# An up projection that goes over from raw to normalised input, two k-tiles a pair of products

## The chip, the cores and the metric

The kernel runs on one core of a Trainium2 chip. The metric is the device time of one execution in microseconds. The kernel before takes 1709.6 us (median of 3 runs, 1709.41 to 1709.67).

## What is computed

One layer of a decoder trunk for 288 tokens: 256 of a prompt and 32 of a sample group (8 sequences of 4). D_MODEL is 2048 and D_FF is 5632. All values are fp32. The part of the reference that the change is in:

```python
x1 = _layernorm(ALPHA * x + mixed @ w_out, ln1_g, ln1_b)
a, b = jnp.split(x1 @ w_up, 2, axis=-1)
a, conv_ffn_new = _causal_dwconv(a, conv_ffn_prev, w_conv_ffn)
y = _layernorm(ALPHA * x1 + (jax.nn.silu(a) * b) @ w_down, ln2_g, ln2_b)
```

What comes ahead of it (one large input projection, a gated short convolution, a dilated window attention, the output projection) is left as it is.

## The kernel before, in words

Features lie on the 128 partitions and tokens on the free axis, so a matrix of 2048 features by 288 tokens is 16 *k-tiles* of 128 x 288. TensorE multiplies in a reduced fp32 type, and each fp32 operand is therefore held as two parts, hi and lo. A *split* makes them: ScalarE (ACT) copies the value to hi, and VectorE (DVE) subtracts hi from the value, which is lo (`split`, one line for all its uses, L231). `mms` (L225 to L227) forms one block of 128 output features: for each of 16 k-tiles it issues three matmuls, hi by hi, hi by lo and lo by hi. Such a block is called a *product* here, of 48 matmuls, in one PSUM accumulator (`acc`, 6 buffers).

Weights stream from HBM, 1 MB a product. They are split in two halves of 8 k-tiles (`whi` by ACT, `wlo` by DVE, 4 buffers each), so that the weights of the next product are split while this one runs. Every engine executes its instructions in one fixed order. That order is not the order of the code: a scheduler makes it when the program is built, and it may put the matmuls of one product among those of its neighbours.

The FFN goes in three parts of 16, 16 and 12 *pairs*. Pair f has two products, a and b, each over the 16 k-tiles of x1: the first product gives a block of `a` (then convolution and Silu), the second a block of `b` (then `gated`: silu(a) times b, and a split of the result into `yah`, `yal`). After the pairs of a part come 16 *down products* that add their share to `dd`.

The layer norm between the mixer and the FFN needs all 16 k-tiles before its mean and variance are known. Part 0 does not wait for it: its 32 products multiply the raw `dd` times the gain g (held split in `xh`, `xl`), with two more columns per k-tile that hold g and b themselves. So a product of part 0 has 290 columns instead of 288 (`x_gb` against `x`). `normed` then applies the norm to the result: an ACT copy of the two extra columns (`wgb`), and two DVE operations (L1011 and L1012) that multiply by r and add the mean's term. Here r and nmr are the per-token factors that `n1.finish` makes.

Meanwhile `dd` itself is normalised in its place, one k-tile a pair: two additions or multiplications on GpSimd (POOL, L1051 and L1052), which `tc.issue_after` puts behind the copies L769 and L770 of that pair, and one on ACT (L1053). In part 0's down products the normalised `dd` is split back into `xh` and `xl`, one k-tile a down product. Parts 1 and 2 then multiply that in 288 columns, with no `normed`.

The steps of a pair, in the names of the trace: first product; ACT `wgb` L1009; DVE `h` L1011, L1012; ACT `u` L1031 (two operations) and `cy` L755; POOL L769, L770 (the last rows, out of `u`), then L1051, L1052 and, for a later pair, L748, L750 (a memset and a copy into `u`); DVE convolution L757 (two); ACT Silu L1037; second product; `wgb`, L1011, L1012 again; DVE `gated` L782, L785; ACT `yah` and DVE `yal`, both L231.

Of the kernel before, what the change touches and what calls it, by code (L numbers as in the profile page):

```python
# [13 lines left out]
AF = mybir.ActivationFunctionType  # L14
ALU = mybir.AluOpType
# [5 lines left out]
KD = D // P  # L21
# [60 lines left out]
TILE_K = 2.5  # L82
VALUES_AT = 64
TILE_V = 2.5
LEAD = 4


# [10 lines left out]
def layer_kernel(ctx: ExitStack, tc: tile.TileContext, ins, outs):  # L98
    nc = tc.nc
    pe, dve, act, pool, sp = nc.tensor, nc.vector, nc.scalar, nc.gpsimd, nc.sync  # L100
# [42 lines left out]
    def behind(i, after):  # L143

        tc.add_manual_dep(i.ins, after.ins.name, no_sync, reason="pace")
# [7 lines left out]
    w_split = []  # L153
# [40 lines left out]
    last_mm = [None]  # L194
# [3 lines left out]
    def prompt_step():  # L198
        if prompt[0]:
            prompt[1] -= 1  # L200
            if prompt[1] <= 0:
                prompt[1] = next(prompt[0], None)
                if prompt[1] is None:
                    prompt[0] = None

    def product(x):
# [8 lines left out]
        mms(o, w, x)  # L215
        prompt_step()
        return o.rearrange("p a h -> p h a")

    def mms(out, w, x):
        nk = sum(n for _, _, n in w)  # L220
        k = 0
        for hi, lo, n in w:
            for c in range(n):
                xh_k, xl_k = (t[:, k].rearrange("p h a -> p a h") for t in x)
                pe.matmul(out, hi[:, c, :], xh_k, start=k == 0, stop=False)  # L225
                pe.matmul(out, hi[:, c, :], xl_k, start=False, stop=False)  # L226
                last_mm[0] = pe.matmul(out, lo[:, c, :], xh_k, start=False, stop=k == nk - 1)  # L227
                k += 1

    def split(hi, lo, src):  # L230
        return act.copy(hi, src), dve.tensor_tensor(lo, src, f32(hi), ALU.subtract)  # L231
# [9 lines left out]
    o = sb(ps, [P, T], "acc")  # L241
# [10 lines left out]
    xs = sb(big, [P, KD, T], "yah")  # L252
# [79 lines left out]
    x = (xh[:, :, :, :H], xl[:, :, :, :H])  # L332
    x_gb = (xh[:, :, :, :HG], xl[:, :, :, :HG])
# [25 lines left out]
    pa = sb(big, [P, KD * T], "yal")  # L359
# [49 lines left out]
    def in_a_row(row):  # L409

        for before, i in zip(row, row[1:]):
            behind(i, before)
# [362 lines left out]
    def gated(out, y, o, add=None):  # L775

        yt = y[:, SEQ : SEQ + NB * (NT + 2)].rearrange("p (b r) -> p b r", b=NB)
        for a, b, c in zip(of_halves(h2(out)), of_tokens(y[:, :SEQ], yt[:, :, 2:]), of_halves(o)):
            if add is None:
                dve.tensor_tensor(a, b, c, ALU.mult)  # L780
            elif len(a.shape) == 3:
                dve.scalar_tensor_tensor(a, c, add, b, ALU.add, ALU.mult)  # L782
            else:
                for h in range(2):
                    dve.scalar_tensor_tensor(a[:, h], c[:, h], add, b[:, h], ALU.add, ALU.mult)  # L785

    cm = sb(big, [P, KD, 2 + 2 * NB], "cm")
    for i in range(KD):
        ph = product(x)
        h = sb(wk, [P, T], "h", bufs=2)  # L790
# [7 lines left out]
        y = conv(u, R_WCM + i * 3)  # L798
# [204 lines left out]
        n1.add(i)  # L1003
    n1.finish()

    def normed(o):
# [4 lines left out]
        dve.tensor_tensor(h2(t), o[:, :, :H], h2(n1.r), ALU.mult)  # L1011
        dve.scalar_tensor_tensor(t, n1.nmr, w[:, 0:1], t, ALU.mult, ALU.add)  # L1012
        return h2(t), w[:, 1:2]
# [3 lines left out]
    f = 0  # L1017
# [3 lines left out]
    for part, nf in enumerate(THIRDS):  # L1021
        gh = sb(big, [P, KD, T], "yah", F32R)
        gl = sb(big, [P, KD, T], "yal", F32R)
        for k in range(nf):
            pa = product(x_gb if part == 0 else x)
            u = sb(wk, [P, UW + 2], "u", bufs=2)
            up, us = conv_in(u[:, :UW], R_SF + f * 2 * NB)
            if part == 0:
                pa, b1 = normed(pa)
                for a, b in zip(of_tokens(up, us), of_halves(pa)):  # L1030
                    act.activation(a, b, AF.Identity, bias=b1)  # L1031
# [5 lines left out]
            act.activation(y, y, AF.Silu)  # L1037
            pb = product(x_gb if part == 0 else x)
            gf = sb(wk, [P, T], "ya", bufs=2)
            if part == 0:  # L1040
                gated(gf, y, *normed(pb))
            else:
                gated(gf, y, pb)
# [4 lines left out]
            if part == 0:  # L1048

                with tc.issue_after(i_rows.ins):  # L1050
                    pool.tensor_tensor(dd[:, k], dd[:, k], n1.r, ALU.mult)  # L1051
                    pool.tensor_tensor(dd[:, k], dd[:, k], n1.nmr, ALU.add)  # L1052
                act.activation(dd[:, k], dd[:, k], AF.Identity, bias=n1.at(n1.b, k), scale=n1.at(n1.g, k))  # L1053
        if f == KF:
            sp.dma_start(outs["o_cf"].rearrange("p (k r) -> p k r", k=KF), cf)
        for i in range(KD):
            o = product((h3(gh), h3(gl)))
            if part == 0:
                for i_x, *before in zip(split(x[0][:, i], x[1][:, i], h2(dd[:, i])), last_split, w_split):
                    for b in before:  # L1060
                        behind(i_x, b)
                dve.scalar_tensor_tensor(h2(dd[:, i]), h2(dd[:, i]), ALPHA, o, ALU.mult, ALU.add)
            else:
                if f == KF and i > 0:
                    i_c = pool.tensor_tensor(dd[:, i], dd[:, i], n2.c, ALU.subtract)
# [197 lines left out]
```

## Time and profile before

| | us |
|---|---|
| three timed runs, median | 1709.6 |
| the profiled execution | 1709.6 |
| its span | 1707.3 |
| TensorE busy in the span | 1700.1 |
| VectorE, ScalarE, GpSimd busy | 1166.9, 912.4, 281.9 |
| part 0, 32 up products (first matmul to last) | 914.93 to 1104.77 |

The profiled execution took what the timed runs took, and 2.3 us of it lie around the span. A profile's TensorE row says how long matmuls were in flight, not how fast they came: a matmul stands for 285 ns in the rows, but one starts every 123 ns, because they are pipelined. In rows of the timeline the columns are start (us from the span's start), duration (us; for a merged row from the first's start to the last's end), engine, line, operation, output<-inputs, shapes and count, and in brackets how long the engine had stood idle and what ended it. Wait rows are: who waited, for whom, us in total, times, longest. A group's row ends in busy us, mean ns of one, and idle time before.

### The profile page before, as it was taken

The page shows a single profiled execution, that of the slowest core. Times are in us where ns is not written, and L with a number is a line of the kernel's source. Part 1 is how long each engine was busy: PE and PEld are TensorE (multiplying, and loading weights), DVE is VectorE, ACT ScalarE, POOL GpSimd, SP SyncE. Part 2 cuts the span into 40 slices and gives each one's busy share as a digit, 9 for nine tenths or more (in the row PEclk, how much of TensorE's full clock was granted, in tenths as well). Part 3 has the DMA queues.
Part 4 walks back from the last instruction along what each step waited for, and adds up shares of the span by engine and source line. Part 5 has one row for each costly group of instructions (what it writes and reads, how often), then busy time and mean ns, then how long its engine had stood idle before and what let it go on. Part 6 is the DMA issues. An engine that isn't in the chain of part 4 may idle for free.

```text
span 1707.3 us, 34051 instructions
## 1 busy us (share of the span) xinstructions
PE 1700.1 (100%) x14110; PEld 1697.4 (99%) x14110; DVE 1166.9 (68%) x1619; ACT 912.4 (53%) x1546; POOL 281.9 (17%) x428
## 2 busy tenths in 40 slices
PE   9999999999999999999999999999999999999998
PEld 9999999999999999999999999999999999999998
DVE  6458998886877675455788888855556555555576
ACT  6356776565655554444546555644455543344455
POOL 0011111000000000011454332300110100011165
PEclk9999999999999999999999999999999999999999
DMA  8766776666767876778766767677677667766663
GB/s 299 281 249 238 255 262 250 233 248 229 258 242 254 312 274 247 266 289 332 272 254 250 261 247 250 249 269 269 249 256 260 248 248 256 274 257 249 246 225 112
DMA packets 61308, 436.19 MB, mean 255 GB/s; under 512 B 7841, under 2 KB 14241, under 8 KB 21537
## 3 DMA queue, kind: packets, MB, share of 16 engines
q1 hardware_dynamic: 59856, 430.19, 68.7%
q10 hardware_dynamic: 1296, 3.83, 0.7%
q8 instruction: 110, 1.80, 0.4%
q14 instruction: 46, 0.37, 0.1%
HBM read 427.53 MB, written 94.53 MB: 306 GB/s over the span
## 4 chain that ended last, share of the span: by engine, by line
PE 99%; DVE 0%; ACT 0%; ACTq 0%; DVEq 0%; issue 0%
PE acc L225 32%; PE acc L226 32%; PE acc L227 32%; PE acc L351 2%; DVE dd L972 0%; PE acc L243 0%; PE acc L621 0%; PE acc L421 0%; PE att L456 0%; PE acc L426 0%; PE att L467 0%; PE att L880 0%; PE att L882 0%; ACT yah L976 0%; ACT cache L941 0%; ACT cache L946 0%
## 5 line engine op out<-in xcount | busy, mean ns | idle before, releaser
L231 DVE TENSOR_TENSOR wlo<-wst,whi 128x1024 fp32r<-128x1024 f32 (+1 forms) x574 | 702.7, 1225 | 420.7 <-ACT whi L231 415.3
L231 ACT CAST whi<-wst 128x1024 fp32r<-128x1024 f32 (+1 forms) x574 | 586.0, 1022 | 707.2 <-PE acc L226 653.4
L225 PE MATMUL acc<-xh,whi 128*128 128x288 f32 (+1 forms) x3184 | 908.0, 285 | 0.0
L226 PE MATMUL acc<-xl,whi 128*128 128x288 f32 (+1 forms) x3184 | 907.7, 285 | 0.0
L227 PE MATMUL acc<-xh,wlo 128*128 128x288 f32 (+1 forms) x3184 | 907.6, 285 | 0.0
L225 PEld LDWEIGHTS acc<-xh,whi 128*128 128x128 f32 x3184 | 599.1, 188 | 0.7 <-issue 0.4
L227 PEld LDWEIGHTS acc<-xh,wlo 128*128 128x128 f32 x3184 | 599.1, 188 | 0.0
L226 PEld LDWEIGHTS acc<-xl,whi 128*128 128x128 f32 x3184 | 598.9, 188 | 0.0
L227 PE MATMUL acc<-yah,wlo 128*128 128x288 f32 x1216 | 347.7, 286 | 0.0
L226 PE MATMUL acc<-yal,whi 128*128 128x288 f32 x1216 | 347.7, 286 | 0.0
L225 PE MATMUL acc<-yah,whi 128*128 128x288 f32 x1216 | 347.6, 286 | 0.0
L227 PEld LDWEIGHTS acc<-yah,wlo 128*128 128x128 f32 x1216 | 229.8, 189 | 0.0
L226 PEld LDWEIGHTS acc<-yal,whi 128*128 128x128 f32 x1216 | 229.8, 189 | 0.0
L225 PEld LDWEIGHTS acc<-yah,whi 128*128 128x128 f32 x1216 | 229.7, 189 | 0.0
L769 POOL COPY qk_s<-u 128x2 f32<-128x2 f32 x44 | 36.6, 832 | 563.6 <-ACT u L1034 442.5
L591 DVE TRANSPOSE_TENSOR_REDUCE sw<-cache 128x32 f32<-128x1024 f32 x64 | 79.5, 1243 | 4.2 <-ACT cache L584 1.1
L757 DVE SCALAR_TENSOR_TENSOR cy<-u,prm,cy 128x304 f32<-128x304 f32 x120 | 71.3, 594 | 3.7 <-ACT cy L755 1.0
L828 POOL TENSOR_TENSOR ya<-ya,dd 128x288 f32<-128x288 f32 x16 | 13.8, 860 | 293.4 <-DVE ya L827 287.8
L231 ACT CAST yah<-ya 128x288 fp32r<-128x288 f32 x76 | 32.5, 428 | 24.8 <-DVE ya L780 8.3
L584 ACT ACTIVATE cache<-cache,qk_s 128x128 f32<-128x128 f32 x128 | 42.9, 392 | 0.0
L584 ACT ACTIVATE cache<-cache,dd 128x128 f32<-128x128 f32 x128 | 42.1, 390 | 0.0
L769 POOL COPY cm<-u 128x2 f32<-128x2 f32 x16 | 7.1, 442 | 198.2 <-DVE u L796 198.2
(219 smaller groups left out, 1106.2 us busy)
## 6 DMA issues: line engine op xcount, KB each, us to landing
wst<-in_w_in SPq DMA_DIRECT2D x111, 1024.0 KB, 4.9
wst<-in_w_up SPq DMA_DIRECT2D x88, 1024.0 KB, 4.9
wst<-in_w_down SPq DMA_DIRECT2D x32, 1024.0 KB, 4.8
cache<-in_ck SPq DMA_DIRECT2D x18, 1024.0 KB, 5.7
cache<-in_cv SPq DMA_DIRECT2D x18, 1024.0 KB, 6.5
wst<-in_w_a SPq DMA_DIRECT2D x16, 1024.0 KB, 5.0
wst<-in_w_out SPq DMA_DIRECT2D x16, 1024.0 KB, 5.0
wst<-in_w_down SPq DMA_DIRECT2D x16, 768.0 KB, 4.5
```

The costliest lines, as they stand in the source:

```text
L225: pe.matmul(out, hi[:, c, :], xh_k, start=k == 0, stop=False)
L226: pe.matmul(out, hi[:, c, :], xl_k, start=False, stop=False)
L227: last_mm[0] = pe.matmul(out, lo[:, c, :], xh_k, start=False, stop=k == nk - 1)
L231: return act.copy(hi, src), dve.tensor_tensor(lo, src, f32(hi), ALU.subtract)
L351: i = pe.matmul(o[b], first_w(term == 2, b, k, 1)[:, 0], xk, start=k == 0 and term == 0, stop=k == KD - 1 and term == 2)
L584: i = act.activation(e_t, e_t, AF.Copy, scale=w[:, g + 1, j, b * NT + t : b * NT + t + 1])
L591: dve.tensor_reduce(parts[:, g, :, j, b * NT : (b + 1) * NT].rearrange("p k j t -> p j t k"), c[:, 2 * half * cols : (2 * half + 2) * cols ...
L757: dve.scalar_tensor_tensor(y, u[:, i : i + YW], prm[:, w0 + i : w0 + i + 1], y, ALU.mult, ALU.add)
L769: pool.tensor_copy(dst[:, 0:2], u[:, SEQ : SEQ + 2])
L828: pool.tensor_tensor(m, m, ma[:, i], ALU.add)
```

## The change

It is all in part 0 of the FFN. Let n be the number of k-tiles that are normalised and split so far.

- `product` and `mms` take a second accumulator. The first n k-tiles of a product multiply the normalised x in 288 columns and sum in the accumulator of their own (`o_first`); the other 16 - n multiply the raw x in 290 columns, as before.
- `up_product` makes a product with the n at hand, applies `normed` to the raw sum, adds the other sum (L1021, one DVE operation), and then splits the k-tiles from n to n_normed into `xh` and `xl`. It does the splits behind the first product of pair f, for n_normed = 2f, so the second product already uses them. From the second product of pair 8 on, all 16 are normalised: products have 288 columns and no `normed`.
- `norm_x` normalises two k-tiles a pair instead of one, in pairs 0 to 7 instead of 0 to 15. Its POOL operations are four in a fixed row, and each k-tile has its ACT operation.
- The 16 splits of x in part 0's down products are gone.

The diff, cut to its core:

```diff
     def mms(out, w, x, first=None, x_first=None, n_first=0):
...
+                o, xs = (first, x_first) if k < n_first else (out, x)
+                xh_k, xl_k = (t[:, k].rearrange("p h a -> p a h") for t in xs)
+                pe.matmul(o, hi[:, c, :], xh_k, start=k in (0, n_first), stop=False)
...
+    def up_product(n_normed):
+        n = n_split[0]
+        if n == KD:
+            return product(x), None
+        o, first = product(x_gb, x, n) if n else (product(x_gb), None)
+        t, b = normed(o)
+        if n:
+            dve.tensor_tensor(t, t, first, ALU.add)
+        for k in range(n, n_normed):
+            split(x[0][:, k], x[1][:, k], h2(dd[:, k]))
+        n_split[0] = max(n, n_normed)
+        return t, b
+
+    def norm_x(ks):
+        row = []
+        for k in ks:
+            row.append(pool.tensor_tensor(dd[:, k], dd[:, k], n1.r, ALU.mult))
+            row.append(pool.tensor_tensor(dd[:, k], dd[:, k], n1.nmr, ALU.add))
+            act.activation(dd[:, k], dd[:, k], AF.Identity, bias=n1.at(n1.b, k), scale=n1.at(n1.g, k))
+        in_a_row(row)
...
-            pa = product(x_gb if part == 0 else x)
+            n_normed = min(PER_PAIR * f, KD)
+            pa, b1 = up_product(n_normed)
...
-            pb = product(x_gb if part == 0 else x)
+            pb, b1 = up_product(n_normed)
...
-            if part == 0:
+            if n_normed < KD:
                 with tc.issue_after(i_rows.ins):
-                    pool.tensor_tensor(dd[:, k], dd[:, k], n1.r, ALU.mult)
-                    pool.tensor_tensor(dd[:, k], dd[:, k], n1.nmr, ALU.add)
-                act.activation(dd[:, k], dd[:, k], AF.Identity, bias=n1.at(n1.b, k), scale=n1.at(n1.g, k))
+                    norm_x(range(n_normed, n_normed + PER_PAIR))
...
             if part == 0:
-                for i_x, *before in zip(split(x[0][:, i], x[1][:, i], h2(dd[:, i])), last_split, w_split):
-                    for b in before:
-                        behind(i_x, b)
```

PER_PAIR is 2. Lines move: L225 to L227 become L230 to L232, the split's L231 becomes L236, L1009, L1011 and L1012 become L1039, L1041 and L1042, L1031 becomes L1061, L1051 and L1052 become L1031 and L1032, L1053 becomes L1033.

Three places of the order, before and after. First TensorE, where the second product of pair 1 begins, with the engines that a matmul waits for. Before (acc_11232 is the pair's first product, acc_11308 its second):

```order
L226 MATMUL acc_11232<-xl_93,whi_11154 128x290
L227 MATMUL acc_11232<-xh_92,wlo_11155 128x290
L225 MATMUL acc_11308<-xh_92,whi_11224 128x290 [waits Activation_49]
L226 MATMUL acc_11308<-xl_93,whi_11224 128x290
L227 MATMUL acc_11308<-xh_92,wlo_11225 128x290 [waits DVE_49]
```

After (acc_11235 is the first product, acc_11316 the normalised and acc_11315 the raw sum of the second):

```order
L231 MATMUL acc_11235<-xl_93,whi_11154 128x290
L232 MATMUL acc_11235<-xh_92,wlo_11155 128x290
L230 MATMUL acc_11316<-xh_92,whi_11227 128x288 [waits PE_49,Activation_49]
L230 MATMUL acc_11315<-xh_92,whi_11227 128x290 [waits PE_49]
L231 MATMUL acc_11315<-xl_93,whi_11227 128x290
L232 MATMUL acc_11315<-xh_92,wlo_11228 128x290 [waits DVE_49]
```

The product now begins with one matmul on the freshly split hi part of k-tile 0; the wait for ACT there is for that split. The rest of k-tile 0 and all of k-tile 1 stand later among the raw ones. In every later second product the new k-tiles stand behind the older normalised ones: behind 6 matmuls in pair 2, behind 42 in pair 8.

Second ACT, where the Silu of pair 0 stands. Before:

```order
L1053 ACTIVATE dd_9931<-dd_9931,prm_221 128x288
L1037 ACT_TABLE_LOAD
L1037 ACTIVATE cy_11143<-cy_11143 128x304
L231 CAST whi_11304<-wst_11298 128x1024
L1009 COPY wgb_11284<-acc_11232 128x2
L231 CAST yah_11069<-ya_11207 128x288
```

After:

```order
L1033 ACTIVATE dd_9931<-dd_9931,prm_221 128x288
L1067 ACT_TABLE_LOAD
L1067 ACTIVATE cy_11143<-cy_11143 128x304
L236 CAST xh_92<-dd_9931 128x2x144
L1033 ACTIVATE dd_9931<-dd_9931,prm_221 128x288
L236 CAST whi_11311<-wst_11305 128x1024
L1039 COPY wgb_11284<-acc_11235 128x2
L236 CAST yah_11069<-ya_11212 128x288
L236 CAST xh_92<-dd_9931 128x2x144
```

The hi split of k-tile 0 stands behind the table load and the Silu, and the norm of k-tile 1 ahead of the next weights' split. Third DVE, from the `gated` of pair 4 to the first `h` of pair 5. Before:

```order
L785 SCALAR_TENSOR_TENSOR ya_11807<-h_11810,wgb_11808,cy_11742 128x16 x2
L231 TENSOR_TENSOR wlo_11901<-wst_11897,whi_11900 128x1024
L231 TENSOR_TENSOR yal_11070<-ya_11807,yah_11069 128x288
L231 TENSOR_TENSOR wlo_11905<-wst_11897,whi_11904 128x1024
L1011 TENSOR_TENSOR h_11885<-acc_11831,cache_9994 128x288
```

After:

```order
L790 SCALAR_TENSOR_TENSOR ya_11854<-h_11850,wgb_11848,cy_11782 128x16 x2
L236 TENSOR_TENSOR wlo_11952<-wst_11948,whi_11951 128x1024
L236 TENSOR_TENSOR xl_93<-dd_9931,xh_92 128x2x144 x2
L236 TENSOR_TENSOR yal_11070<-ya_11854,yah_11069 128x288
L236 TENSOR_TENSOR wlo_11956<-wst_11948,whi_11955 128x1024
L1041 TENSOR_TENSOR h_11928<-acc_11876,cache_9994 128x288
```

The two lo splits of x now stand ahead of the next pair's `h`. On ACT the row of the same pair is: both norms L1033, one weight split, both hi splits of x, `yah`, the other weight split. On POOL it is: L774, L775, then L1031, L1032, L1031, the memset and copy L753 and L755, and the last L1032.

More of the change, by code (lines that the diff above doesn't have):

```diff
@@ L84 @@
 TILE_V = 2.5
+PER_PAIR = 2
 LEAD = 4
@@ L204, in prompt_step, with product @@
                     prompt[0] = None
-    def product(x):
+    def product(x, x_first=None, n_first=0):
         w = w_ready.pop(0)
@@ L214, in product, with mms @@
         o = acc(x[0].shape[-1])
-        mms(o, w, x)
+        o_first = acc() if n_first else None
+        mms(o, w, x, o_first, x_first, n_first)
         prompt_step()
+        if n_first:
+            return o.rearrange("p a h -> p h a"), o_first.rearrange("p a h -> p h a")
         return o.rearrange("p a h -> p h a")
-    def mms(out, w, x):
+    def mms(out, w, x, first=None, x_first=None, n_first=0):
         nk = sum(n for _, _, n in w)
@@ L223, in mms @@
             for c in range(n):
[L224 to L227, printed above, removed]
+                o, xs = (first, x_first) if k < n_first else (out, x)
+                xh_k, xl_k = (t[:, k].rearrange("p h a -> p a h") for t in xs)
+                pe.matmul(o, hi[:, c, :], xh_k, start=k in (0, n_first), stop=False)
+                pe.matmul(o, hi[:, c, :], xl_k, start=False, stop=False)
+                last_mm[0] = pe.matmul(o, lo[:, c, :], xh_k, start=False, stop=k in (n_first - 1, nk - 1))
                 k += 1
@@ L1004, in layer_kernel @@
     n1.finish()
+    n_split = [0]
+    def up_product(n_normed):
[17 more added lines that the diff above has]
+        in_a_row(row)
     def normed(o):
@@ L1024, in layer_kernel @@
         for k in range(nf):
-            pa = product(x_gb if part == 0 else x)
+            n_normed = min(PER_PAIR * f, KD)
+            pa, b1 = up_product(n_normed)
             u = sb(wk, [P, UW + 2], "u", bufs=2)
             up, us = conv_in(u[:, :UW], R_SF + f * 2 * NB)
-            if part == 0:
-                pa, b1 = normed(pa)
+            if b1 is not None:
                 for a, b in zip(of_tokens(up, us), of_halves(pa)):
@@ L1037, in layer_kernel @@
             act.activation(y, y, AF.Silu)
-            pb = product(x_gb if part == 0 else x)
+            pb, b1 = up_product(n_normed)
             gf = sb(wk, [P, T], "ya", bufs=2)
[L1040 to L1043, printed above, removed]
+            gated(gf, y, pb, b1)
             last_split = split(gh[:, k], gl[:, k], gf)
@@ L1047, in layer_kernel @@
                 next(rows, None)
-            if part == 0:
+            if n_normed < KD:
                 with tc.issue_after(i_rows.ins):
-                    pool.tensor_tensor(dd[:, k], dd[:, k], n1.r, ALU.mult)
-                    pool.tensor_tensor(dd[:, k], dd[:, k], n1.nmr, ALU.add)
-                act.activation(dd[:, k], dd[:, k], AF.Identity, bias=n1.at(n1.b, k), scale=n1.at(n1.g, k))
+                    norm_x(range(n_normed, n_normed + PER_PAIR))
         if f == KF:
```

## The prediction

> **What bounds the kernel now.** I read the page first, then the waits, the groups by form, and part 0 of the FFN row by row. From the page:
>
> ```profile
> span 1707.3 us, 34051 instructions
> ...
> PE 1700.1 (100%) x14110; PEld 1697.4 (99%) x14110; DVE 1166.9 (68%) x1619; ACT 912.4 (53%) x1546; POOL 281.9 (17%) x428
> ```
>
> TensorE works all through; next to nothing is left to win in its waits. The waits of PE say the same: two rows, 1.6 us in all, neither of them in the up products.
>
> ```profile
> PE acc L243 <- DVE cy L240: 1.2, 1, 1.2
> ...
> PE acc L955 <- DVE dd L972: 0.4, 1, 0.4
> ```
>
> So there are two ways to a change of the time: matmuls that come faster, or a wait of TensorE that is not there now. For the second I look at one pair of part 0, 11.80 us long. The columns are PE, PEld, DVE, ACT and POOL busy (operations), granted clock, DMA share, GB/s:
>
> ```profile
> 956.40:968.20 11.80, 11.80 (x98) 11.80 (x97) 9.58 (x15) 6.92 (x12) 4.08 (x6) 1.00 0.71 267
> ```
>
> VectorE is busy 9.58 of 11.80 us, so there are 2.2 us to spare, but only if its work can be done in any order, which it can't: each engine's order is fixed.
>
> **The gain: 288 columns for 290.** How fast matmuls come is read from their starts. The first and the last row of 165 with 290 columns, and of 166 with 288 in part 1:
>
> ```profile
> 929.76 0.29 PE L227 MATMUL acc<-xh,wlo 128*128 128x290 f32 x1
> ...
> 949.99 0.29 PE L226 MATMUL acc<-xl,whi 128*128 128x290 f32 x1
> ```
>
> ```profile
> 1299.73 0.29 PE L225 MATMUL acc<-xh,whi 128*128 128x288 f32 x1
> ...
> 1319.95 0.28 PE L225 MATMUL acc<-xh,whi 128*128 128x288 f32 x1
> ```
>
> 20.23 us by 164 steps is 123.35 ns; 20.22 by 165 is 122.55 ns. That is 0.8 ns for two columns. The groups have 512 matmuls of each of the three lines with 290 columns, 1536 in all:
>
> ```profile
> L226 PE MATMUL acc<-xl,whi 128*128 128x290 f32 x512 | 146.9, 287 | 0.0
> ```
>
> After the change, products with n normalised k-tiles keep 48 - 3n of them: n is 0 twice (first and second of pair 0), and once more in the first of pair 1, then 2, 2, 4, 4 and so on up to 14, 14, and from there 16. That leaves 144 + 2 x 3 x (14 + 12 + 10 + 8 + 6 + 4 + 2) = 480, so 1056 matmuls lose two columns: 1056 x 0.8 ns = **0.85 us**, all of it on the path. Bounds: nothing, if starts go by something other than columns, and 1056 x 2.1 ns = 2.2 us, if I had taken the difference of mean durations (287 against 285).
>
> **What goes.** 16 splits of x leave the down products of part 0, 15 products lose `normed` (L1011, L1012, an ACT copy). TensorE never waits there, so this is worth nothing. SP's order and the DMAs are the same. A second accumulator takes two of six buffers a product; one is read within a product's time and is needed again two products later: nothing.
>
> **What comes: a loop of waits through four engines.** The splits of x come up into the pairs. Seven pairs on TensorE now wait for `xl` of k-tiles that were normalised one pair earlier. The normalisation starts behind POOL's copies of `u`, which start behind the pair's first `h`; and the next pair's first `h` stands on VectorE behind those two `xl` (the third order view). So each pair's L1041 follows the L1041 of the pair before by the sum of everything between, a loop whose length I can add up from rows. VectorE and ACT:
>
> ```profile
> 959.19 0.45 DVE L1011 TENSOR_TENSOR h<-acc,cache 128x288 f32<-128x288 f32 x1
> 959.68 0.52 DVE L1012 SCALAR_TENSOR_TENSOR h<-cache,wgb,h 128x288 f32<-128x288 f32 x1
> ...
> 967.31 1.22 DVE L231 TENSOR_TENSOR wlo<-wst,whi 128x1024 fp32r<-128x1024 f32 x1
> ```
>
> ```profile
> 960.88 0.74 ACT L1031 ACTIVATE u<-h,wgb 128x256 f32<-128x256 f32 x2
> ...
> 964.52 0.63 ACT L1053 ACTIVATE dd<-dd,prm 128x288 f32<-128x288 f32 x1 [0.17 <-POOL dd L1052]
> 965.85 1.05 ACT L231 CAST whi<-wst 128x1024 fp32r<-128x1024 f32 x1 [0.70 <-PE acc L226]
> 967.43 0.43 ACT L231 CAST yah<-ya 128x288 fp32r<-128x288 f32 x1 [0.53 <-DVE ya L785]
> ```
>
> And POOL:
>
> ```profile
> 961.48 0.80 POOL L769 COPY qk_s<-u 128x2 f32<-128x2 f32 x1 [7.68 <-ACT u L1031]
> 962.22 0.19 POOL L770 COPY qk_s<-u 128x16 f32<-128x16 f32 x1
> 962.38 1.13 POOL L1051 TENSOR_TENSOR dd<-dd,cache 128x288 f32<-128x288 f32 x1
> 963.58 0.91 POOL L1052 TENSOR_TENSOR dd<-dd,cache 128x288 f32<-128x288 f32 x1
> 964.44 0.09 POOL L748 MEMSET u<- 128x2 f32 x1
> 964.48 1.16 POOL L750 COPY u<-prm 128x16 f32<-128x16 f32 x1
> ```
>
> The x splits themselves have rows in the down products:
>
> ```profile
> L231 DVE TENSOR_TENSOR xl<-dd,xh x16: 449/452/455, 1110.9 to 1195.4; 128x288 fp32r<-128x288 f32 x16
> ```
>
> The loop from pair 5 on: L1041 and L1042 0.45 + 0.52, the new addition L1021 0.45 (never run; nearest row is L1011, also PSUM and SBUF in), with a hand-off 1.47. From the start of `u` to the end of the first k-tile's L1052, 960.88 to 964.49, 3.61. The second k-tile's two, with memset and copy between them, 1.13 + 1.20 + 0.91 and hand-offs: 3.3. Its ACT norm 0.63. Then ACT's row: a weight split 1.05, two `xh` 0.86 (as `yah`, 0.43 each), `yah` 0.43, the other weight split 1.05; VectorE's `wlo` 1.22 ends it: 4.61. Together 1.47 + 3.61 + 3.3 + 0.63 + 4.61 = **13.6 us**. TensorE needs 11.8 for a pair, and in each pair the new k-tiles stand 6 matmuls (0.74 us) later in the product. So TensorE falls behind by 13.6 - 11.8 - 0.74 = 1.1 us a pair, and waits for it.
>
> How it starts is seen at pair 1. Its second product begins where this matmul is, 144 and some of the window attention's behind the first of part 0:
>
> ```profile
> 933.22 0.29 PE L225 MATMUL acc<-xh,whi 128*128 128x290 f32 x1
> ```
>
> ```profile
> 931.69 0.63 ACT L1053 ACTIVATE dd<-dd,prm 128x288 f32<-128x288 f32 x1 [0.31 <-POOL dd L1052]
> 932.33 1.28 ACT L1037 ACT_TABLE_LOAD   x1
> 933.63 0.46 ACT L1037 ACTIVATE cy<-cy 128x304 f32<-128x304 f32 x1
> ```
>
> ```profile
> 936.20 0.45 DVE L1011 TENSOR_TENSOR h<-acc,cache 128x288 f32<-128x288 f32 x1
> ```
>
> k-tile 0 is normalised in time, but its `xh` stands behind table load and Silu (second order view): 934.09 + 0.43 = 934.5, a wait of 1.3 us for the first matmul. The second norm, weight split and `wlo` then take pair 1's L1041 from 936.2 to 934.5 + 0.63 + 1.05 + 1.22 = 937.4. From there I followed each engine's row with the durations above. Pair 5, for one: the second norm of the loop ends 1.47 + 3.61 + 3.3 + 0.63 behind pair 4's L1041 of 977.6, at 986.6; the weight split at 987.65, `xh` at 988.1, `wlo` at 988.9, the first `xl` at 989.3. The product began at 985.0 and comes to that k-tile 24 matmuls later, at 987.95: it waits 1.35. All pairs, in us from the span's start:
>
> | pair | first L1041 | second product starts | waits in it, us |
> |---|---|---|---|
> | 1 | 937.4 | 933.2 | 1.3 (`xh` of k-tile 0) |
> | 2 | 951.7 | 946.3 | 0.85 |
> | 3 | 963.6 | 959.0 | 0.55 |
> | 4 | 977.6 | 971.3 | 1.85 |
> | 5 | 991.2 | 985.0 | 1.35 |
> | 6 | 1004.8 | 998.1 | 1.1 |
> | 7 | 1018.4 | 1011.0 | 1.5 |
> | 8 | | 1024.3 | 2.5 |
>
> Pairs 2 and 3 wait less because ACT does one k-tile's norm and split ahead of the other's there. Pair 8 waits more because its second `xl` stands behind a `wlo` (1.22) and the next L1041 (0.45) as well. The sum is 11.0 us. After pair 8 nothing new is awaited, and a bound engine doesn't make lost time good. Against 0.85 won: **+10.1 us on the profiled run's 1709.6 (equal to the median; 1707.3 of span and 2.3 around it): 1719.7 us.**
>
> **What the loop's rows are uncertain in.** Where POOL and VectorE work side by side, both have long and short forms (least, median, most, in ns):
>
> ```profile
> L1051 POOL TENSOR_TENSOR dd<-dd,cache x16: 789/1127/1134, 929.9 to 1104.5; 128x288 f32<-128x288 f32 x16
> ```
>
> ```profile
> L750 POOL COPY u<-prm x60: 197/202/1208, 48.2 to 1596.7; 128x16 f32<-128x16 f32 x60
> ```
>
> ```profile
> L757 DVE SCALAR_TENSOR_TENSOR cy<-u,prm,cy x120: 491/534/1182, 247.5 to 1619.0; 128x304 f32<-128x304 f32 x120
> ```
>
> ```profile
> L990 POOL TENSOR_TENSOR h<-xh,xl x16: 800/1782/1797, 814.9 to 904.7; 128x288 f32<-128x288 f32 x16
> ```
>
> Short: two L1031 at 0.79 and the copy at 0.20 take 2 x 0.34 + 0.96 = 1.6 off the loop, to 12.0. Long: four POOL additions at 1.78 add 2 x 0.65 + 2 x 0.87 = 3.0, to 16.6. I take the middle rows, since they are the form that these very operations have in part 0 (1.13 is the median of its row).
>
> For this the Trainium skill has a rule, in SBUF — State Buffer, section Who interferes with whom: a VectorE instruction with two SBUF inputs and a GpSimd instruction that reads SBUF share a read interface, which the one that came first holds for its whole instruction. It speaks against this change, which adds two two-input subtractions and two POOL operations to every pair. The trace's two-valued rows agree with it, but do not show who held the port; by the rule in full the loop goes to the long end, by the middle rows it stays at 13.6.
>
> **The rivals.**
> *The loop is short (1710.6).* If POOL's rows are short, 12.0 is less than 11.8 + 0.74: nothing piles up, pair 1's wait stays, with about half a microsecond in pair 2; 1709.6 + 1.3 + 0.5 - 0.85 = 1710.6, no slower than before by what can be told (0.2%, 3.4 us, is about what a measurement of this kernel can tell from no change). It decides at a loop of 12.5. Against it are the copies L750 of part 0, the first and the last of 16:
>
> ```profile
> 932.58 1.03 POOL L750 COPY u<-prm 128x16 f32<-128x16 f32 x1
> ...
> 1106.56 1.15 POOL L750 COPY u<-prm 128x16 f32<-128x16 f32 x1
> ```
>
>
> *All splits hidden (1708.8).* Only the 0.85 us shows. Against it the first wait, which no size of POOL's rows changes.
> *Contention at the long end (1740).* Loop 16.6: 3.0 more in each of seven pairs, 1719.7 + 21 = 1740.7. VectorE's 9.58 us a pair, with 1.8 for two `xl` and two L1021, come to 11.4 and near the whole pair, so POOL seldom finds it idle; L1051 never took 1.78.
> *The clock falls.* A dip to half the clock for some microseconds would cost as many again. The window row grants 1.00, and my waits are each under 2.6 us, so none here should; with one or two dips that cost 3 us each the time would be about 1725 (a guess at their number; no row shows a dip).
>
> The Trainium skill, TensorE: Matmul & The Clock Gate, Part 1: The HAM clock gate, has TensorE fall to half its clock after an idle window of about 3.4 us. No run of before has such a wait.
>
> **How the numbers follow.** The loop as added up, .71 (1714 to 1729); the short loop .16 (1709.5 to 1713); all hidden .02; contention .06; the clock .03; .02 for a gain that the trace doesn't show. The range goes from 1711.5, inside the short loop, to 1730, which takes in twice the wait that I expect per pair, and leaves out contention's far end. Faster by over 0.2% is the last .02, the same is .16 + .02, slower .71 + .06 + .03.
>
> **What will show it.** Right: waits of PE for ACT `xh` and DVE `xl` at eight places from 934 on, about 1.3 at the first; L1041 of successive pairs 13 to 14 us apart; no wait behind pair 8. Wrong: pairs of 11.8 us throughout (the loop is short), POOL rows of 1.7, or a clock under 1.00. A saving of over 3.4 us would overturn the pitch of 0.8 ns.

## The result and the profile after

| | before | after |
|---|---|---|
| median, us (14 runs each) | 1709.47 | 1712.84 |
| lowest to highest | 1709.14 to 1709.73 | 1712.25 to 1713.38 |
| span of the profiled execution | 1707.3 | 1710.9 |

The ratio is 1.002, with a 95% interval from 1.0013 to 1.0027: slower by 3.4 us. The forecast was 10.1 us. The time lies inside the range (1711.5 to 1730), near its low end, and the size is a third of what was expected. That the range holds it is luck: its low end was set for a shorter loop of waits, and the cost that 1719.7 rested on did not come (see below).

The page after has the same matmuls; TensorE is now busy for 99% of the span:

```profile
span 1710.9 us, 34005 instructions
...
PE 1700.8 (99%) x14110; PEld 1697.0 (99%) x14110; DVE 1155.7 (68%) x1595; ACT 906.9 (53%) x1531; POOL 274.1 (16%) x428
```

The waits of PE after, in the form of the two rows of before. Both old rows are still there, and two are new, for the operations that the prediction named:

```profile
PE acc L231 <- DVE xl L236: 1.8, 3, 1.2
PE acc L248 <- DVE cy L245: 1.2, 1, 1.2
PE acc L230 <- ACT xh L236: 1.1, 1, 1.1
PE acc L960 <- DVE dd L977: 0.4, 1, 0.4
```

The two new rows say 2.9 us, and this is not the whole loss. The timeline of PE around pair 1's wait, around pair 3's, and around the last one:

```profile
934.60 0.51 PE L230 MATMUL acc<-xh,whi 128*128 128x288 f32 x2 [1.08 <-ACT xh L236]
934.95 0.28 PE L231 MATMUL acc<-xl,whi 128*128 128x290 f32 x1
...
961.06 0.29 PE L230 MATMUL acc<-xh,whi 128*128 128x290 f32 x1
961.64 0.39 PE L231 MATMUL acc<-xl,whi 128*128 128x288 f32 x1 [0.29 <-DVE xl L236]
961.86 0.29 PE L232 MATMUL acc<-xh,wlo 128*128 128x288 f32 x1
...
1024.26 0.28 PE L230 MATMUL acc<-xh,whi 128*128 128x288 f32 x1
1025.70 0.39 PE L231 MATMUL acc<-xl,whi 128*128 128x288 f32 x1 [1.16 <-DVE xl L236]
1025.93 0.29 PE L232 MATMUL acc<-xh,wlo 128*128 128x288 f32 x1
```

The reader should go by starts. From 1024.26 to 1025.70 is 1.44 us where 0.12 is usual, and the next start comes 0.23 later, which is 0.10 too much again: this wait costs 1.42, though its bracket has 1.16. (A bracket counts from the end of the matmul before, which stands for 0.285 us in the rows, and so it is 0.16 short of the late start.) Counted so, by every start that came late:

| pair | forecast, us | measured, us |
|---|---|---|
| 1 | 1.3 | 1.35 |
| 2 | 0.85 | 0 |
| 3 | 0.55 | 0.56 |
| 4 | 1.85 | 0.59 |
| 5, 6, 7 | 1.35, 1.1, 1.5 | 0.04, 0, 0.20 |
| 8 | 2.5 | 1.42 |
| sum | 11.0 | 4.17 |

4.17 less the 0.85 of the 288 columns is 3.32; measured are 3.37. The traces show that nothing behind part 0 has moved: from part 0's first matmul to the first of its down products (914.93 to 1104.89 before, 915.06 to 1108.42 after) it is 3.4 us more, and what follows takes 602.45 us in both. What was forecast too large is the waits of pair 2 and of pairs 4 to 8, so the loop. That pair 3 agrees is luck: its first `h` came 1.0 us earlier than forecast (962.64 for 963.6), and TensorE had lost 0.8 us less by then. The loop's length is the distance of the pairs' first L1041:

```profile
975.40 0.45 DVE L1041 TENSOR_TENSOR h<-acc,cache 128x288 f32<-128x288 f32 x1
...
987.87 0.45 DVE L1041 TENSOR_TENSOR h<-acc,cache 128x288 f32<-128x288 f32 x1
```

12.47 us, and 12.44 in the two pairs behind it, where 13.6 was forecast. TensorE can bear 11.8 + 0.74 = 12.54. The windows between these operations, columns as in the prediction's window row:

```profile
975.40:987.87 12.47, 12.47 (x104) 12.47 (x103) 11.78 (x20) 7.91 (x16) 5.15 (x8) 1.00 0.48 168
987.87:1000.31 12.44, 12.44 (x104) 12.44 (x103) 11.77 (x20) 7.78 (x15) 5.16 (x8) 1.00 0.68 254
```

PE is busy throughout, at a clock of 1.00, and VectorE for 11.78 of 12.47 us, against 9.58 of 11.80 before.

### The profile page after: what moved, and what is told of

Same layout as the page of the kernel before. It is cut to its first block, busy times and chain, and to the rows that moved or that the text cites. A ratio compares the mean times of both kernels' runs of the same rounds, so it can differ in the third digit from the quotient of the medians.

```text
span 1710.9 us, 34005 instructions
## 1 busy us (share of the span) xinstructions
PE 1700.8 (99%) x14110; PEld 1697.0 (99%) x14110; DVE 1155.7 (68%) x1595; ACT 906.9 (53%) x1531; POOL 274.1 (16%) x428
## 4 chain that ended last, share of the span: by engine, by line
PE 95%; DVE 3%; ACT 1%; issue 1%; POOL 0%; ACTq 0%; DVEq 0%; POOLq 0%
PE acc L230 31%; PE acc L231 31%; PE acc L232 31%; PE acc L356 2%; DVE wlo L236 1%; DVE dd L977 0%; PE acc L248 0%; DVE h L1042 0%; DVE xl L236 0%; DVE h L1021 0%; PE acc L626 0%; DVE h L1041 0%; ACT u L1061 0%; DVE cy L762 0%; PE acc L426 0%
## 5 line engine op out<-in xcount | busy, mean ns | idle before, releaser
L236 DVE TENSOR_TENSOR wlo<-wst,whi 128x1024 fp32r<-128x1024 f32 (+1 forms) x574 | 701.7, 1224 | 426.8 <-ACT whi L236 421.7
L236 ACT CAST whi<-wst 128x1024 fp32r<-128x1024 f32 (+1 forms) x574 | 585.4, 1021 | 694.2 <-PE acc L231 639.5
L231 PE MATMUL acc<-xl,whi 128*128 128x288 f32 (+1 forms) x3184 | 907.5, 285 | 1.8 <-DVE xl L236 1.8
L230 PE MATMUL acc<-xh,whi 128*128 128x288 f32 (+1 forms) x3184 | 906.7, 285 | 1.1 <-ACT xh L236 1.1
L232 PE MATMUL acc<-xh,wlo 128*128 128x288 f32 (+1 forms) x3184 | 906.8, 285 | 0.0
L231 PEld LDWEIGHTS acc<-xl,whi 128*128 128x128 f32 x3184 | 598.7, 188 | 2.6 <-DVE xl L236 2.4
L230 PEld LDWEIGHTS acc<-xh,whi 128*128 128x128 f32 x3184 | 598.5, 188 | 2.0 <-ACT xh L236 1.3
L232 PEld LDWEIGHTS acc<-xh,wlo 128*128 128x128 f32 x3184 | 598.9, 188 | 0.0
L232 PE MATMUL acc<-yah,wlo 128*128 128x288 f32 x1216 | 347.9, 286 | 0.0
L231 PE MATMUL acc<-yal,whi 128*128 128x288 f32 x1216 | 347.9, 286 | 0.0
L230 PE MATMUL acc<-yah,whi 128*128 128x288 f32 x1216 | 347.8, 286 | 0.0
L232 PEld LDWEIGHTS acc<-yah,wlo 128*128 128x128 f32 x1216 | 229.9, 189 | 0.0
L230 PEld LDWEIGHTS acc<-yah,whi 128*128 128x128 f32 x1216 | 229.9, 189 | 0.0
L231 PEld LDWEIGHTS acc<-yal,whi 128*128 128x128 f32 x1216 | 229.9, 189 | 0.0
L774 POOL COPY qk_s<-u 128x2 f32<-128x2 f32 x44 | 34.7, 789 | 571.1 <-ACT u L1064 506.3
L785 DVE TENSOR_TENSOR ya<-cy,acc 128x256 f32<-128x256 f32 x104 | 27.5, 305 | 28.5 <-PE acc L232 28.4
L236 ACT CAST yah<-ya 128x288 fp32r<-128x288 f32 x76 | 32.4, 427 | 18.9 <-DVE ya L785 9.4
```

Source lines behind the costliest of these rows:

```text
L230: pe.matmul(o, hi[:, c, :], xh_k, start=k in (0, n_first), stop=False)
L231: pe.matmul(o, hi[:, c, :], xl_k, start=False, stop=False)
L232: last_mm[0] = pe.matmul(o, lo[:, c, :], xh_k, start=False, stop=k in (n_first - 1, nk - 1))
L774: pool.tensor_copy(dst[:, 0:2], u[:, SEQ : SEQ + 2])
```

## The experiments

Each kernel of an experiment ran beside the kernel before on the same chip, 7 to 11 runs against 15 to 33. "Late starts" is the sum of what PE's matmuls in part 0 start late, from the trace of the run; 0.8 ns for each matmul with 288 columns is taken off it, and the result is set beside the measured difference of the medians.

| run | late starts | columns | together | measured | ratio, 95% interval |
|---|---|---|---|---|---|
| the change | 4.17 | -0.85 | +3.32 | +3.37 | 1.0013 to 1.0027 |
| e1_no_split | 0 | -0.85 | -0.85 | -0.78 | 0.9987 to 1.0004 |
| e2_half_pair | 2.64 | -0.81 | +1.83 | +1.80 | 1.0001 to 1.0019 |
| e3_one_k | 1.35 | -0.54 | +0.81 | +0.82 | 0.9996 to 1.0014 |
| e6_pair_later | 2.71 | -0.77 | +1.94 | +1.89 | 1.0001 to 1.0019 |
| e7_norm_later | 0.74 | -0.81 | -0.07 | +0.05 | 0.9991 to 1.0009 |
| e5_u_behind | 3.68 | -0.85 | +2.83 | +2.96 | 1.0008 to 1.0026 |
| e4_pool_half | 6.12 | -0.85 | +5.27 | +5.05 | 1.0018 to 1.0040 |
| e4_pool_more | 5.22 | -0.85 | +4.37 | +4.05 | 1.0014 to 1.0033 |
| e9_no_second_add | 4.03 | -0.85 | +3.18 | +3.30 | 1.0009 to 1.0027 |
| e10_no_pool_norm | 0 | -0.85 | -0.85 | -1.16 | 0.9984 to 1.0002 |
| e8_one_k_later | 0 | -0.50 | -0.50 | -0.06 | 0.9989 to 1.0007 |
| e11_pair_later_each | 0 | -0.77 | -0.77 | -0.56 | 0.9987 to 1.0006 |

The columns "together" and "measured" agree to 0.45 us or better in all, which is less than the intervals tell apart (0.0009 is 1.5 us). The traces say it more closely: part 0, from its first matmul to the first of its down products, differs from the 189.97 us of before by the column "together" to about 0.1 us in every kernel, and what follows takes 602.44 to 602.56 us in all. So what the change does to the time is matmul starts in part 0; what remains is why the starts are late.

**Is it the splits alone?** Theory: pitch and waits for xh and xl make up the whole difference.

```diff
-        for k in range(n, n_normed):
-            split(x[0][:, k], x[1][:, k], h2(dd[:, k]))
```

> The changed kernel with the splits of x left out (the normalised k-tiles never go into xh and xl, so all products go on with the raw x; the two accumulators, the 288 columns, L1021 and the norms stay). Theory (the whole difference is matmul pitch plus TensorE's waits for xh and xl): no wait in the up products of part 0, and 1056 x 0.8 ns = 0.85 us less than before: 1708.6 us. Rival 1 (288 columns bring nothing here): 1709.5. Rival 2 (the second accumulator, L1021 or the norms two a pair also hold TensorE up): 1710 to 1712, with waits for something other than xh and xl.

Measured 1708.69 against 1709.47, with no late start in part 0. The second accumulators and L1021 hold nothing up. The interval of the ratio holds 1, so the medians alone do not show the gain of 0.78; the trace does: part 0 takes 189.17 us for 189.97, 0.80 less, where 0.85 was forecast.

**The first wait.** Two kernels. The first has one k-tile a pair, with the last split behind the pairs:

```diff
-PER_PAIR = 2
+PER_PAIR = 1
...
+        for k in range(n_split[0], KD):
+            split(x[0][:, k], x[1][:, k], h2(dd[:, k]))
+        n_split[0] = KD
         for i in range(KD):
             o = product((h3(gh), h3(gl)))
```

The second starts one pair later:

```diff
-            n_normed = min(PER_PAIR * f, KD)
+            n_normed = min(PER_PAIR * max(f - 1, 0), KD)
...
-            if n_normed < KD:
+            if f > 1 and n_normed < KD:
```

> The changed kernel with one k-tile a pair instead of two (the last is split behind the last pair). 675 matmuls have 288 columns: -0.54 us. Theory: each loop loses two POOL operations, a norm, an xh and an xl, some 3.5 of its 12.45 us, so only the wait of pair 1 stays (its xh stands behind the table load and the Silu, 1.35 us with the slow matmul behind it): 1709.5 + 1.35 - 0.54 = 1710.3 us. Rival (waits come from load, not from the loop): half the load, half of the 4.17 us of waits, 1709.5 + 2.1 - 0.54 = 1711.1, spread over several pairs.

> The changed kernel with the norms and splits begun one pair later (k-tiles 0 and 1 normalised in pair 1, split in pair 2), all else alike. 960 matmuls have 288 columns: -0.77 us. Theory: the wait for xh of k-tile 0 (1.35 us in the changed kernel) goes, since no table load stands ahead of it in pair 2; the others stay about as they are, shifted by a pair (2.8 us): 1709.5 + 2.8 - 0.77 = 1711.5 us. Rival (the first wait is the lateness of POOL's norms, not the table load): it stays, 1712.9.

1710.29 and 1711.36. With one k-tile a pair, pair 1's 1.35 us are the only late starts; with the later start they go but for 0.19. So pair 1's wait is the place behind the table load, as forecast. ACT in the changed kernel has the norm of k-tile 0 done at 932.46, and its `xh` only behind table load and Silu; the matmul that waits starts at 934.60:

```profile
931.83 0.63 ACT L1033 ACTIVATE dd<-dd,prm 128x288 f32<-128x288 f32 x1 [0.31 <-POOL dd L1032]
932.47 1.28 ACT L1067 ACT_TABLE_LOAD   x1
933.76 0.46 ACT L1067 ACTIVATE cy<-cy 128x304 f32<-128x304 f32 x1
934.13 0.41 ACT L236 CAST xh<-dd 128x288 fp32r<-128x288 f32 x1
```

The order changes a little with each such edit, so the small waits are not the same ones.

**Half a pair of room.** The splits behind the second product:

```diff
-            pa, b1 = up_product(n_normed)
+            pa, b1 = up_product(0)
```

> The changed kernel with each pair's splits put behind its second product instead of its first: they are used half a pair (5.9 us) later. 1008 matmuls have 288 columns instead of 1056. Theory (a loop of waits from one first h to the next through xl, and lateness at single places): the xl no longer stand ahead of the next h with a norm that has just ended, no wait of TensorE for xh or xl, 1709.5 - 0.81 = 1708.7 us. Rival (the additional load on VectorE and the shared time of POOL and VectorE hold TensorE up, wherever the splits stand): 1711.5 to 1713.

1711.27: a miss. Late starts of 2.6 us stay, and the first h are still 12.2 us apart, although no fresh xl stands ahead of them. My next theory was that the loop closes on ACT, where the norms stand ahead of the weight splits. This run has the same edit, and puts them behind both:

```diff
-            act.activation(dd[:, k], dd[:, k], AF.Identity, bias=n1.at(n1.b, k), scale=n1.at(n1.g, k))
         in_a_row(row)
...
         for k in range(n, n_normed):
+            i_n = act.activation(dd[:, k], dd[:, k], AF.Identity, bias=n1.at(n1.b, k), scale=n1.at(n1.g, k))
+            behind(i_n, w_split[0])
             split(x[0][:, k], x[1][:, k], h2(dd[:, k]))
```

> The kernel of the run with splits half a pair later, with one thing more: ACT's two norms of a pair stand behind both weight splits that they stood ahead of. Theory (the loop from one first h to the next closes through ACT: norm, weight split, wlo, next h; the splits of x only lie beside it): the first h come 11.8 us apart instead of 12.2 to 12.35, no wait of TensorE for xh or xl, 1709.5 - 0.81 = 1708.7 us. Rival (the loop closes through xl, or load on VectorE decides): the 2.6 us of waits stay, 1711.3.

1709.54: 1.7 us better than the run before, and yet the theory fell, since the first h did not come any closer. The windows from one to the next, in this kernel:

```profile
972.46:984.67 12.21, 12.21 (x102) 12.21 (x101) 11.93 (x19) 7.78 (x16) 5.39 (x8) 1.00 0.47 178
984.67:996.85 12.18, 12.18 (x101) 12.18 (x100) 11.90 (x19) 7.77 (x16) 5.62 (x8) 1.00 0.69 258
```

VectorE is busy for 11.9 of 12.2 us. No engine holds it up any more by more than a few hundredths: it is itself the loop, a row of operations that takes longer than TensorE's 11.8. That the late starts fell all the same fits the first pairs, which began less late: from pair 0's first `h` to pair 2's it is 21.1 us, and 22.8 in the run before.

**What fills VectorE.** Its work before, 9.57, with two xl (0.82) and two L1021 (0.90) comes to 11.3, which would fit into 11.8. Left out here are POOL's four operations of a pair's norms:

```diff
-            row.append(pool.tensor_tensor(dd[:, k], dd[:, k], n1.r, ALU.mult))
-            row.append(pool.tensor_tensor(dd[:, k], dd[:, k], n1.nmr, ALU.add))
```

> The changed kernel with POOL's four operations of a norm left out (ACT's part and the splits stay, on values without r and nmr). The chain loses some 3.5 us, and VectorE's rows, 9.57 us before and 11.77 now, lose what POOL's operations stretch them by: I take 0.5 to 0.9. Theory (POOL's row costs by the chain and by stretching VectorE): first h 11.8 us apart, only pair 1's wait of 1.35 and up to 0.5 in pair 8: 1709.5 + 1.35 + 0.3 - 0.85 = 1710.3 us. Rival (the two xl and the two L1021 alone fill VectorE): first h stay over 12.1 apart and the time at 1712.

1708.23, no late start at all. VectorE's window of a pair, and its two convolution operations, in this kernel:

```profile
976.73:988.53 11.80, 11.80 (x98) 11.80 (x97) 10.46 (x20) 6.95 (x13) 1.16 (x4) 1.00 0.73 268
```

```profile
985.73 1.11 DVE L762 SCALAR_TENSOR_TENSOR cy<-u,prm,cy 128x304 f32<-128x304 f32 x2
```

And VectorE in the changed kernel, where POOL's row runs beside it:

```profile
978.45 1.86 DVE L762 SCALAR_TENSOR_TENSOR cy<-u,prm,cy 128x304 f32<-128x304 f32 x2 [0.41 <-ACT cy L760]
980.23 1.81 DVE L236 TENSOR_TENSOR wlo<-wst,whi 128x1024 fp32r<-128x1024 f32 x1
...
982.45 0.72 DVE L1042 SCALAR_TENSOR_TENSOR h<-cache,wgb,h 128x288 f32<-128x288 f32 x1
```

1.86 against 1.11 for the convolution, 1.81 against 1.23 for a wlo, 0.72 against 0.52: POOL's norms stretch VectorE's row by 1.3 us a pair (11.78 against 10.46). I had expected 0.5 to 0.9. Not all of it is new. The kernel before, with one k-tile's norm a pair, already has the long forms:

```profile
962.31 1.52 DVE L757 SCALAR_TENSOR_TENSOR cy<-u,prm,cy 128x304 f32<-128x304 f32 x2
963.97 1.61 DVE L231 TENSOR_TENSOR wlo<-wst,whi 128x1024 fp32r<-128x1024 f32 x1
```

So some 0.8 of the 1.3 us lie within the 9.57 of before, and the change adds 0.5 (11.78 against the 11.3 above). Pair 1's wait went as well; without POOL's row ahead of them ACT does norms and xh before the table load. The stretch agrees with the Trainium skill, SBUF — State Buffer, section Who interferes with whom, by which a VectorE instruction with two SBUF inputs and a GpSimd instruction that reads SBUF share a port: all three stretched rows have two SBUF inputs. In the prediction I looked for the price on POOL; what the change adds is on VectorE.

**Is POOL's chain a limit too?** In the changed kernel, the chain through u, POOL, ACT's norm and the weight split could be just as long as VectorE's row, 12.45. Four kernels ask. One takes an operation out of VectorE's row that the chain doesn't have:

```diff
-        if n:
+        if n and add:
             dve.tensor_tensor(t, t, first, ALU.add)
...
-            pb, b1 = up_product(n_normed)
+            pb, b1 = up_product(n_normed, False)
```

> The changed kernel without L1021 in the second product of each pair (its b is then short of the normalised share). The operation lies in VectorE's row of a pair, and not in the chain from first h through u, POOL, ACT's norm, weight split and wlo to the next first h. Theory (two limits lie together at about 12.45 us a pair, VectorE's full row and that chain): first h of pairs 4 to 7 stay 12.35 to 12.45 apart and the time between 1712 and 1713. Rival (VectorE's row alone): 12.0 apart, waits of pairs 3, 4 and 8 smaller, 1711.5 us.

1712.69, and the first h stay 12.46 apart while VectorE's busy time falls to 11.4:

```profile
974.94:987.40 12.46, 12.46 (x104) 12.46 (x103) 11.40 (x19) 7.89 (x16) 5.16 (x8) 1.00 0.50 170
```

So the chain is a limit of its own, at 12.46. Two kernels make it longer, with a further addition on half of every second k-tile (here), or on all of it (the same line without the `: T // 2`):

```diff
             row.append(pool.tensor_tensor(dd[:, k], dd[:, k], n1.nmr, ALU.add))
+            if k % 2:
+                row.append(pool.tensor_tensor(dd[:, k, : T // 2], dd[:, k, : T // 2], n1.nmr[:, : T // 2], ALU.add))
```

> The changed kernel with a further POOL addition on half of every second k-tile (144 columns, some 0.45 us; x then has nmr added twice in that half). In pairs 5 to 8 the rows of ACT are as in the changed kernel. Theory: the loop of 12.45 goes to about 12.95, over 11.8 + 0.74 = 12.54, so pairs 5 to 7, which now wait 0 to 0.2 us each, wait about 0.4 each, and pair 8 as much more: about +1.7, 1714.5 us (1713.5 to 1716). Rival (POOL's rows are not in the chain that TensorE waits for): 1712.8.

> The same with the further POOL addition on the whole of every second k-tile (0.87 us; nmr is added twice there). Here the order of ACT changes too: the weight split stands between the two norms and no longer behind both. Theory: the loop gains 0.87 and loses that weight split (0.94), so it stays at about 12.4, and the time at 1712.9 us (1712 to 1714) although POOL does twice as much more as in the half dose. Rival (each us of POOL's row counts by itself): 7 x 0.8 = +5.6, 1718.4.

1714.54 and 1713.54: the small dose costs more than the large one, as the chain says, since with the large one the weight split leaves the chain. The windows of the half dose and of the whole:

```profile
987.54:1000.65 13.11, 12.79 (x105) 12.58 (x104) 11.91 (x19) 7.78 (x15) 5.75 (x9) 1.00 0.64 240
```

```profile
988.79:1001.22 12.43, 12.43 (x104) 12.43 (x103) 11.77 (x19) 7.76 (x15) 6.06 (x9) 1.00 0.66 253
```

13.11 is over 12.54, and TensorE waits in each of pairs 6 and 7; 12.43 is under it, with POOL busier than in any other run. With the large dose VectorE's row is the limit alone: its `wlo` starts at 997.84, when the weight split that it needs has long been done (994.60 to 995.63). So VectorE's row by itself, with its wait of 0.4 for ACT's `cy`, takes 12.43, and the chain by itself, in the run before these two, 12.46. The last one makes the chain shorter:

```diff
-        pool.memset(u[:, 0:2], 0.0)
+        i_u = pool.memset(u[:, 0:2], 0.0)
+        if norm_last[0] is not None:
+            behind(i_u, norm_last[0])
```

> The changed kernel with POOL's memset and copy into u put behind the last norm of the row instead of ahead of it. Theory: the loop loses about 1.1 us of its 12.45, first h come 11.8 us apart, the waits of pairs 3 and 4 (1.15 us) go, that of pair 1 (1.35) stays, pair 8's falls from 1.42 to 0 to 0.7: 1709.5 + 1.35 + 0.3 - 0.85 = 1710.3 us. Rival (the waits are the places of single splits, not the loop's length): 1712.8 as the changed kernel.

1712.45, a miss: the first h are 12.30 apart and not 11.8. POOL's last addition, which now follows at once, in this kernel:

```profile
980.72 1.66 POOL L1036 TENSOR_TENSOR dd<-dd,cache 128x288 f32<-128x288 f32 x1
```

It takes 1.66 us, where behind the copy it took 0.79, and ends only 0.2 us earlier in the pair. It runs beside VectorE's wlo (979.91 to 981.73). So most of what the copy seemed to cost was, as it looks, time that POOL would have waited for VectorE anyway.

**A version without late starts.** One is e7 with `PER_PAIR = 1` and the last split behind the pairs. The other has two k-tiles a pair, the norm at the split as in e7, and both a whole pair later:

```diff
-            pa, b1 = up_product(n_normed)
+            pa, b1 = up_product(min(PER_PAIR * (f - 1), KD))
...
-            pb, b1 = up_product(n_normed)
+            pb, b1 = up_product(0)
```

> One k-tile a pair, its split half a pair later, and ACT's norm behind both weight splits: what the runs so far point to for a kernel without any wait. 630 matmuls have 288 columns: 1709.5 - 0.50 = 1709.0 us, no wait of TensorE in part 0. Rival (something else of the change costs): 1709.5 or more, with a wait of TensorE in part 0 to name it.

> Two k-tiles a pair, but ACT's norm and the splits of each k-tile come a whole pair later than in the changed kernel, behind the first product of the pair after next, and are used from its second product on. 960 matmuls have 288 columns: 1709.4 - 0.77 = 1708.6 us if TensorE waits for no xh or xl. VectorE's rows may still be 12.2 us a pair; seven pairs of that make it late by 7 x 0.4 = 2.8 us, less than the half pair (5.9 us) that is to spare. Rival (VectorE's full row reaches TensorE all the same): waits for xl in the last pairs, 1709.3 or more.

1709.33 against 1709.39, and 1708.81 against 1709.37; neither has a late start in part 0. The second is the fastest complete kernel here: 0.56 us faster than before (1708.34 to 1709.28 against 1709.01 to 1709.84), where the change is 3.37 slower. The interval of its ratio, 0.9987 to 1.0006, holds 1; its part 0 takes 189.25 us for 189.97. Its rows are no shorter, 12.43 us a pair:

```profile
983.30:995.73 12.43, 12.43 (x103) 12.43 (x102) 11.76 (x19) 8.70 (x16) 5.17 (x8) 1.00 0.66 253
```

So VectorE falls behind by 0.6 us a pair as in the change, but here the splits have a pair to spare, and no matmul starts late.

## Why the prediction was right or wrong

- *The bound, and the gain of 0.85 us*: right. e1 has 0.78 by the medians and 0.80 in the trace, and the sums of all runs close with 0.8 ns a matmul.
- *Work taken away that is worth nothing (normed, the splits in the down products), accumulators*: right by e1, whose time needs no further term.
- *Pair 1's wait, 1.3 us*: right in size (1.35) and cause.
- *The loop of 13.6 us*: wrong, and this is the step that failed. Its five terms, as the prediction put them and as the trace after has them from 975.40 on:

| term | forecast | measured |
|---|---|---|
| L1041, L1042, L1021, hand-off | 1.47 | 1.60 |
| u to the end of the first k-tile's L1032 | 3.61 | 2.98 |
| the second k-tile's, with memset and copy | 3.3 | 2.87 |
| ACT's norm | 0.63 | 0.66 |
| ACT's row and wlo | 4.61 | 4.36 |
| sum | 13.6 | 12.47 |

  The rows behind the second and third term, POOL after:

```profile
977.62 0.46 POOL L774 COPY qk_s<-u 128x2 f32<-128x2 f32 x1 [7.31 <-ACT u L1061]
...
978.18 0.80 POOL L1031 TENSOR_TENSOR dd<-dd,cache 128x288 f32<-128x288 f32 x1
979.06 0.92 POOL L1032 TENSOR_TENSOR dd<-dd,cache 128x288 f32<-128x288 f32 x1
979.93 1.03 POOL L1031 TENSOR_TENSOR dd<-dd,cache 128x288 f32<-128x288 f32 x1
...
980.95 1.15 POOL L755 COPY u<-prm 128x16 f32<-128x16 f32 x1
982.06 0.79 POOL L1032 TENSOR_TENSOR dd<-dd,cache 128x288 f32<-128x288 f32 x1
```

  0.46 and 0.80 stand where I took 0.80 and 1.13: I called 1.13 the form of these operations in part 0, and in the new order the first came in its short form. The second k-tile's rows, too, are each somewhat shorter than I took them. This is the larger part of the error: the two POOL terms are 1.06 us too long, some 0.9 of it by forms. ACT's rows show the other mistake:

```profile
982.88 0.63 ACT L1033 ACTIVATE dd<-dd,prm 128x288 f32<-128x288 f32 x1 [1.57 <-POOL dd L1032]
983.42 1.03 ACT L236 CAST whi<-wst 128x1024 fp32r<-128x1024 f32 x1
984.35 0.76 ACT L236 CAST xh<-dd 128x288 fp32r<-128x288 f32 x2
985.02 0.43 ACT L236 CAST yah<-ya 128x288 fp32r<-128x288 f32 x1
985.35 1.04 ACT L236 CAST whi<-wst 128x1024 fp32r<-128x1024 f32 x1
```

  Each starts 0.09 or 0.10 before the end of the one ahead of it, so a chain must be added from start to start, and I added durations. The rows of before showed that already. (The Trainium skill, ScalarE: Activation LUTs, section What ACT_TABLE_LOAD costs, says that back-to-back ACTIVATEs overlap by about 93 ns; the trace agrees, with 0.09.) This is most of the 0.25 that the last term is too long; with that term alone put right the loop would still have come to 13.4. Altogether an error of 1.15 us in 13.6 is 8%, but it lies across the point of 12.54 from which the loop decides: over it by 1.1, TensorE would have waited in every pair; in truth it is under it by 0.1, and only the uneven pairs at the beginning and the end show.
- *Pair 8's wait*: right in place: its second `xl` stands behind a `wlo` and the next L1041, as forecast. It cost 1.42 instead of 2.5, which fits the lateness that was to arrive there and had not piled up.
- *VectorE as cover*: wrong in an instructive way. The prediction noted 11.4 us of work for VectorE and did not make it a limit. It is 11.78 with what POOL stretches, and alone, with the chain gone (e7), it makes a row of 12.2.
- *The rivals*: "the loop is short" came nearest in mechanism: its steady pairs wait as it says, next to not at all. It was given a chance of .16, with the loop that would decide it (12.5) and the short forms of POOL's rows (12.0) worked out. Its price, 1710.6, lacked the waits of pairs 3, 4 and 8. The long end of contention and a falling clock did not come.

What stays open: in the changed kernel VectorE's row (12.43 alone) and the chain (12.46 alone) lie within a few hundredths of each other, and no run separates their shares in the uneven pairs 3 and 4.

## What to carry to other kernels

When a chain of waits has to be compared with a budget, add it from start to start, take each row's short and long form, and give the sum's distance to the point of decision with its error: here the error, 1.15 us, was more than ten times that distance. A side engine that is 20% idle is not free cover if its order is fixed and another engine slows it; its own row is a loop that must fit too. If work for later is prepared along a bound engine's loop, a whole turn of slack cost almost nothing here (e11: 96 matmuls fewer with 288 columns, 0.08 us) and took the lateness out of the sum.

## What the runs showed of the hardware

- A wait of TensorE costs about 0.10 us more than itself: the matmul behind one that waited starts 0.226 to 0.228 us after it, where 0.122 is usual, in all but a few of the shortest waits (37 of 42 late starts in the runs' part 0). In the changed kernel this is 0.5 of the 4.17 us, and no row of waits has it.
- POOL and VectorE side by side cost both. VectorE paid 0.75 us on two convolution operations and 0.58 on a wlo. POOL's additions were no longer than before (0.79 to 1.03 us), except where one ran straight into a wlo (1.66 instead of 0.79, e5). Its small copy L755 took 1.15 us, as before (1.16), and ended at 982.10, just behind the wlo that ended at 982.04; in e10, with nothing of VectorE beside it, it took 0.20:

```profile
987.02 0.20 POOL L755 COPY u<-prm 128x16 f32<-128x16 f32 x1
```

- Two columns less on a matmul of 290 are 0.8 ns a start, and 1056 of them made part 0 0.80 us shorter when nothing else moved (e1).
